# Attention scores of a decoder layer: two products of 128 rows per head, or three of 64 rows in paired halves of TensorE

## The chip, the cores and the metric

The kernel runs on one core of one Trainium2 chip. A core has TensorE (PE in the profile, with its weight loads listed as PEld), VectorE (DVE), ScalarE (ACT), GpSimd (POOL) and SyncE (SP), which issues most of the DMAs. The time is device microseconds of one execution, and the number that counts is the median over runs.

## The reference: what is computed

One decoder layer over 2048 positions of width 1024, in float32. Attention has 8 query heads of 64 and 2 key heads, each of which serves a group of 4 query heads; the window is 128 positions, and each head has a learned sink.

```python
h = rms_norm(x, attn_norm_g[l])
z = h @ w_in[l]
...
q = rms_norm(q, q_norm_g[l])
k = rms_norm(k, k_norm_g[l])
y_attn = swa_sink_attention(q, k, v, sinks[l])
y_conv = gate_b * short_conv(gate_c * xc, conv_w[l])
y = jnp.concatenate([rms_norm(y_attn, attn_out_g[l]),
                     rms_norm(y_conv, conv_out_g[l])], axis=-1)
x = x + y @ w_out[l]
hm = rms_norm(x, mlp_norm_g[l])
x = x + jnp.square(jax.nn.relu(hm @ w_up[l])) @ w_down[l]
```

Inside the attention, with blocks of 128 positions, the scores of a block of queries run over its own keys and those of the block before:

```python
sc = jnp.einsum('bnqhgd,bnkhd->bnhgqk', qb, kw).astype(jnp.float32) * scale
mask = (delta >= 0) & (delta < WINDOW) & (kpos[:, None, :] >= 0)
sc = jnp.where(mask[None, :, None, None], sc, NEG_INF)
```

## The kernel before

The products run on numbers of the type float32r. To keep the accuracy of float32, each operand is split into a high part (a copy in float32r) and a low part (what is left), and a product is a sum of part products: high by high, high by low, low by high. The helper `mm3` (lines 278 to 280) does that for the projections, with three products of 128 rows each.

The layer has two halves. In the first, the *mixers*, four chunks of 512 positions (`mixers`, each with four blocks of 128 positions) go through the input projection, attention, the convolution and the output projection. In the second, the MLP runs as Strassen products (lines 1454 and 1571); the diff does not touch it.

What a block does, in this order:

- `project_qkv` (for chunk 0, `first_chunk`) writes the projection `z` of its rows: 512 columns of q, 128 of k, 128 of v. The copy from PSUM is line 663 (line 627 for chunk 0).
- `qk_norm` normalises q and k.
- `qk_transpose` turns four 128x128 pieces of q into one bank (line 697) and k into another (line 699). A piece of q holds two heads that lie side by side, so both belong to the same key group, one on rows 0 to 63 and one on rows 64 to 127. Lines 702 and 703 make a tile `qt` in which every head has all 128 rows: its high part on one half, its low part on the other. Lines 704 to 707 do the same for k, in two arrangements (high over low, and low over high), for both key groups, in the tile `kw`, which keeps the own block and the one before.
- `softmax` makes the scores (line 724). Per pair of heads there is one bank; per head, two products of all 128 rows, one with each arrangement of k, and their sum holds all four part products. That is 16 products per block and 256 over the 16 blocks. They have 256 columns (own block and the one before), in block 0 128 columns. Line 732 copies the own half on ACT, line 735 puts the other block's scores where the mask says so, on DVE. Lines 737 to 749 are the softmax.
- `values` turns the probabilities (line 760) and multiplies them with v (line 812).

Attention's small products have other work beside them: `besides` is a generator of convolution, projection and normalisation steps for the same chunk and the next. `fill(n)` takes n steps of it, and the table FILL says how many stand between two parts of a block; PRIO gives parts a higher or lower rank. The framework's scheduler then sets the order of each engine's queue, by ranks and by its own costs, and that order is fixed in the program. In chunks 0 and 2 (blocks 0 to 3 and 8 to 11) the score products of a block stand together in TensorE's queue; in chunks 1 and 3 they stand one by one between the projections' products.

PSUM has eight banks: three for projections ("mm"), four that attention takes in turn ("at"), and one for turning ("tr").

Of the kernel before, what the change touches and what calls it, by code (L numbers as in the profile page):

```python
# [7 lines left out]
F32 = mybir.dt.float32  # L8
F32R = mybir.dt.float32r
BF16 = mybir.dt.bfloat16  # L10
I32 = mybir.dt.int32
AF = mybir.ActivationFunctionType
ALU = mybir.AluOpType
# [3 lines left out]
P = 128  # L17
# [3 lines left out]
HEADS, KVH, DH = 8, 2, 64  # L21
GQ = HEADS // KVH
AW = HEADS * DH
# [81 lines left out]
def hymba_layer(  # L105
# [19 lines left out]
    nc = tc.nc  # L125
# [30 lines left out]
    def bank(tag, name):  # L156
        return psum.tile([P, 512], F32, tag=tag, name=name, bufs=BANKS[tag])
# [5 lines left out]
    def zrow(name):  # L163

        return pool.tile([P, O_B], F32, tag="z", name=name, bufs=NT)


    ident = const.tile([P, P], F32, name="ident")
    mhalf = const.tile([P, 16], F32, name="mhalf")
# [3 lines left out]
        ident, ident, pattern=[[-1, P]], compare_op=ALU.is_equal, fill=0.0, base=0, channel_multiplier=1  # L173
# [3 lines left out]
    later = const.tile([P, P], I32, name="later")  # L177
    nc.gpsimd.memset(later, 1)
    nc.gpsimd.affine_select(
        later, later, pattern=[[1, P]], compare_op=ALU.is_gt, fill=0.0, base=0, channel_multiplier=-1  # L180
    )
    neg = const.tile([P, 1], F32, name="neg")
# [93 lines left out]
    def mm3(ps, st, mv, first, last):  # L276

        nc.tensor.matmul(ps, st(0), mv(0), start=first, stop=False)  # L278
        nc.tensor.matmul(ps, st(0), mv(1), start=False, stop=False)  # L279
        last_sum[0] = nc.tensor.matmul(ps, st(1), mv(0), start=False, stop=last).ins  # L280
# [116 lines left out]
    def parts(pool_, tag, name):  # L397
        return [pool_.tile([P, KD, CH], F32R, tag=f"{tag}{s}", name=f"{tag}{s}_{name}", bufs=1) for s in range(2)]
# [73 lines left out]
    z0 = [zrow(f"z0_{t}") for t in range(NT)]  # L472
# [3 lines left out]
    h = parts(pool, "h", "a0")  # L476
# [3 lines left out]
    rs0, rs0_2 = rs0_both[:, 0], rs0_both[:, 1]  # L480
# [37 lines left out]
    def first_chunk(first):  # L518
# [68 lines left out]
        pzs = [bank(tag, f"pz0_0_{t}") for t, tag in enumerate(("mm", "mm", "mm", "tr"))]  # L587
# [26 lines left out]
        for i in range(4):  # L614
            r = slice(i * 512, (i + 1) * 512)
# [3 lines left out]
        keep_q(0)  # L619
        w4 = [w.rearrange("p (k c) -> p k c", k=KD) for w in hl]  # L620
        for t in range(NT):
            nc.scalar.activation(z0[t][:, :AW], pzs[t], AF.Copy, scale=rs0[:, t : t + 1])
        for t in range(NT):
            ps = bank("at", f"pz0_1_{t}")[:, :256]
            hk = lambda s, k, t=t: h[s][:, k, t * P : (t + 1) * P]
# [7 lines left out]
    with tc.tile_pool(name="first", bufs=1) as first:  # L633
        with tc.manual_schedule(engines={ET.PE, ET.Activation, ET.DVE, ET.Pool, ET.SP}):
            rs0_in = first_chunk(first)

    with tc.tile_pool(name="mix_small", bufs=1) as mix_small, tc.tile_pool(name="mix", bufs=1) as mix:

        kw = mix.tile([P, 2, KVH, 2, P], F32R, name="kw")
        vz = mix.tile([P, 2, KVH, 2, 2, DH], F32R, name="vz")

        vd = mix.tile([P, KVH, 2, 2, DH], F32R, name="vd")
# [3 lines left out]
        def project_qkv(c, h, z):  # L648

            z += [zrow(f"z{c}_{t}") for t in range(NT)]  # L650
            both = [[by_k(w) for w in weights(None, c, f"q{half}")] for half in range(2)]
            w4 = [w.rearrange("p (k c) -> p k c", k=KD) for w in weights(None, c, "qkv2")]

            for pc, t in ((0, 0), (0, 1), (1, 0), (0, 2), (0, 3), (1, 1), (1, 2), (1, 3)):
                n = 256 if pc else AW
                ps = bank("mm", f"pz{c}_{pc}_{t}")[:, :n]
                hk = lambda s, k, t=t: h[s][:, k, t * P : (t + 1) * P]
                wk = (lambda s, k: w4[s][:, k, :]) if pc else (lambda s, k: both[k // (KD // 2)][s][:, k % (KD // 2), :])
                for k in range(KD):
                    mm3(ps, lambda s, k=k: hk(s, k), lambda s, k=k: wk(s, k), k == 0, k == KD - 1)  # L660
                    if (k % 2 or not pc) and k < KD - 1:
                        yield
                nc.scalar.copy(z[t][:, pc * AW : pc * AW + n], ps)
                if pc and not t:
                    qk_norm(c * NT, z[0])
                yield
# [22 lines left out]
        def qk_transpose(b, zt):  # L689

            nm = f"b{b}"
            own = b % 2
            lo, hi = slice(0, DH), slice(DH, P)
            qt = mix.tile([P, HEADS // 2, 2, P], F32R, tag="qt", name=f"qt_{nm}", bufs=1)
            pt = bank("at", f"ptq_{nm}")
            for j in range(4):
                nc.tensor.transpose(pt[:, j * P : (j + 1) * P], zt[:, j * P : (j + 1) * P], ident)
            pk = bank("at", f"ptk_{nm}")[:, :P]
            nc.tensor.transpose(pk, zt[:, O_K:O_V], ident)
            p3 = pt.rearrange("p (j q) -> p j q", j=4)  # L700
            for i, (a, o) in enumerate(((lo, hi), (hi, lo))):
                nc.scalar.copy(qt[a, :, i, :], p3[a])
                nc.vector.tensor_tensor(qt[o, :, i, :], p3[a], qt[a, :, i, :].bitcast(F32), op=ALU.subtract)
                nc.scalar.copy(kw[a, i, i, own, :], pk[a])
                nc.scalar.copy(kw[o, 1 - i, i, own, :], pk[a])
                nc.vector.tensor_tensor(kw[o, i, i, own, :], pk[a], kw[a, i, i, own, :].bitcast(F32), op=ALU.subtract)
                nc.vector.tensor_tensor(
                    kw[a, 1 - i, i, own, :], pk[a], kw[a, i, i, own, :].bitcast(F32), op=ALU.subtract
                )
            return qt  # L710

        def softmax(b, qt):


            nm = f"b{b}"
            nk = (2 if b else 1) * P
            own = b % 2
            sc = mix.tile([P, HEADS, P], F32, tag="sc", name=f"sc_{nm}", bufs=2)
            for pr in range(HEADS // 2):
                kv = pr * 2 // GQ  # L720
                ps = bank("at", f"psc_{nm}_{pr}").rearrange("p (h s k) -> p h s k", h=2, s=2)
                for j in range(2):
                    for r in range(2):
                        nc.tensor.matmul(  # L724
                            ps[:, j].rearrange("p s k -> p (s k)")[:, :nk],
                            qt[:, pr, j, :],
                            kw[:, r, kv, :, :].rearrange("p s k -> p (s k)")[:, :nk],
                            start=r == 0,
                            stop=r == 1,
                        )  # L730
                s2 = sc[:, pr * 2 : pr * 2 + 2, :]
                nc.scalar.copy(s2, ps[:, :, own, :])  # L732
                for j in range(2):
                    other = ps[:, j, 1 - own, :] if b else neg.to_broadcast([P, P])
                    nc.vector.copy_predicated(s2[:, j, :], later, other)  # L735
            ngm = mix_small.tile([P, HEADS], F32, tag="ngm", name=f"ngm_{nm}", bufs=2)
            nc.vector.tensor_reduce(ngm, sc, axis=AX.X, op=ALU.max, negate=True)
            nc.vector.tensor_tensor(ngm, ngm, nsink, op=ALU.min)  # L738
            den = mix_small.tile([P, HEADS], F32, tag="den", name=f"den_{nm}", bufs=2)
            for hd in range(HEADS):  # L740
                nc.scalar.activation(  # L741
                    sc[:, hd, :], sc[:, hd, :], AF.Exp, bias=ngm[:, hd : hd + 1], accum_out=den[:, hd : hd + 1]
                )
            es = mix_small.tile([P, HEADS], F32, tag="es", name=f"es_{nm}", bufs=2)
            nc.vector.tensor_tensor(es, sink, ngm, op=ALU.add)
            nc.scalar.activation(es, es, AF.Exp)
            nc.vector.tensor_tensor(den, den, es, op=ALU.add)
            nc.vector.reciprocal(den, den)
            nc.vector.tensor_tensor(sc, sc, den[:, :, None].to_broadcast([P, HEADS, P]), op=ALU.mult)
            return sc  # L750
# [227 lines left out]
        def besides(c, before, h, yt, rc, x1, h_next, z_next):  # L978
# [47 lines left out]
            if c + 1 < NCHUNK:  # L1026
                yield from project_qkv(c + 1, h_next, z_next)
            else:
                begin_mlp()
# [62 lines left out]
        z = z0  # L1092
# [6 lines left out]
        pr = bank("at", "pr")  # L1099
# [15 lines left out]
        for c in range(NCHUNK):  # L1115
            left, h, z = mixers(c, left, h, z)
# [215 lines left out]
    wts, ps, vs = {}, {}, {}  # L1332
# [105 lines left out]
    for i, (n, p) in enumerate(seq):  # L1438
# [12 lines left out]
        pt = ps[n, p if p in GOES_ON else AFTER.get(p)]  # L1451
        for k in range(NB):
            for j, (a, b) in enumerate(((0, 0), (0, 1), (1, 0))):
# [4 lines left out]
                    start=p not in GOES_ON and k + j == 0,  # L1458
                    stop=k + j == NB + 1,
# [93 lines left out]
    ps, vs = {}, {tb: {} for tb in range(NTB)}  # L1553

    later = []
    for i, (p, g) in enumerate(steps):
# [5 lines left out]
        for tb in range(NTB):  # L1562
            if first and p not in GOES_ON:
                ps[tb] = banks(tb, f"d{p}_{tb}")
            for j in range(NB):
# [3 lines left out]
                for k, n, cs in sums:  # L1569
                    a, b = ((0, 0), (0, 1), (1, 0))[n]  # L1570
# [4 lines left out]
                        start=first and p not in GOES_ON and k + n == 0,  # L1575
                        stop=last and k + n == 3,
# [34 lines left out]
```

## Time and profile before

The profile is of one execution; its span goes from the first to the last instruction. Each row of a view that shows a group of instructions has the line, the engine, what is written from what, the shapes, the count, and the busy time with the mean of one.

| | before |
|---|---|
| median of three runs | 1917.67 us (1916.55 to 1918.78) |
| span of the profiled execution | 1913.4 us |
| PE busy, granted clock | 1907.7 us, 1.00 |
| mixers, from the start to about | 690 us |
| products of the MLP | 609.7 + 609.5 us busy |
| score products (line 724) | 256, busy 49.0 us with overlaps |
| DVE, ACT, POOL busy | 1202.7, 829.4, 274.4 us |

TensorE is the engine to look at. [...] The other engines are idle for a third of the span and more.

### The profile page before, as it was taken

What the parts mean: (1) busy time and instruction counts of PE and PEld (TensorE: products, weight loads), DVE (VectorE), ACT (ScalarE), POOL (GpSimd) and SP (SyncE); (2) the same over time, 40 slices, a digit from 0 to 9 for tenths busy, and PEclk for the clock granted to TensorE, in tenths of its full rate; (3) what the DMA queues carried; (4) which work ended last, traced back from release to release, by engine and by line L of the source; (5) the groups of instructions that cost most, each with busy time, mean ns of one, the idle gap of its engine ahead of it and who ended that gap; (6) DMA issues with size and microseconds to landing.
All of it is one profiled execution on the core that took longest, in us unless ns stands there. A gap on an engine that the chain in (4) does not pass through costs nothing.

```text
span 1913.4 us, 24557 instructions
## 1 busy us (share of the span) xinstructions
PE 1907.7 (100%) x8930; PEld 1591.1 (83%) x8930; DVE 1202.7 (63%) x1857; ACT 829.4 (43%) x1557; POOL 274.4 (14%) x477
## 2 busy tenths in 40 slices
PE   9999999999999999999999999999999999999999
PEld 8888888888888888888888888888888888888887
DVE  5895567448467759998788766666534334457531
ACT  6564245335445346544555545453332332232320
POOL 2123212302221112233101111111000000100000
PEclk9999999999999999999999999999999999999999
DMA  9984844564578688777576544448954457766631
GB/s 305 333 320 120 329 189 177 213 227 160 203 266 277 215 294 251 221 215 244 195 233 213 175 145 159 140 148 321 364 198 150 138 171 224 281 228 213 217 124 55
DMA packets 232792, 413.80 MB, mean 216 GB/s; under 512 B 51672, under 2 KB 136416, under 8 KB 219872
## 3 DMA queue, kind: packets, MB, share of 16 engines
q1 hardware_dynamic: 203840, 336.59, 52.0%
q0 software_dynamic: 15424, 51.40, 6.9%
q10 hardware_dynamic: 13408, 24.26, 3.4%
q8 instruction: 70, 1.15, 0.2%
q14 instruction: 50, 0.41, 0.1%
HBM read 286.35 MB, written 125.83 MB: 215 GB/s over the span
## 4 chain that ended last, share of the span: by engine, by line
PE 99%; DVE 0%; POOL 0%; issue 0%; ACT 0%; DVEq 0%; POOLq 0%
PE u L1454 32%; PE d L1571 32%; PE pout L278 3%; PE pout L280 3%; PE pout L279 3%; PE pz L278 2%; PE pz L280 2%; PE pz L279 2%; PE psc_b L724 2%; PE pb_c L280 2%; PE pb_c L279 2%; PE pb_c L278 2%; PE px_c L278 2%; PE px_c L279 2%; PE px_c L280 2%; PE po_b L812 1%
## 5 line engine op out<-in xcount | busy, mean ns | idle before, releaser
L1454 PE MATMUL u<-op_x,wop 128*128 128x512 f32 x2688 | 609.7, 389 | 0.0
L1571 PE MATMUL d<-op_w,op_f 128*128 128x512 f32 x2691 | 609.5, 389 | 0.0
L1571 PEld LDWEIGHTS d<-op_w,op_f 128*128 128x128 f32 x2691 | 504.8, 188 | 104.7
L1454 PEld LDWEIGHTS u<-op_x,wop 128*128 128x128 f32 x2688 | 504.3, 188 | 105.3 <-issue 0.3
L434 DVE TENSOR_TENSOR op_f<-op_f 128x1024 fp32r<-128x1024 f32 x112 | 136.8, 1224 | 235.6 <-ACT op_f L433 235.4
L433 ACT CAST op_f<-op_f 128x1024 fp32r<-128x1024 f32 x112 | 117.7, 1051 | 349.5 <-DMA op_f<-fop 349.0
L452 ACT CAST wop<-wu 128x512 fp32r<-128x512 f32 x156 | 96.1, 619 | 92.0 <-PE u L1454 88.3
L453 DVE TENSOR_TENSOR wop<-wu,wop 128x512 fp32r<-128x512 f32 x156 | 110.2, 708 | 31.8 <-ACT wop L452 16.7
L1190 POOL DMA_DIRECT2D fop<-s x96 | 52.1, 542 | 443.2 <-DVE s L1193 436.7
L1196 DVE TENSOR_TENSOR u<-u,u 128x512 f32<-128x512 f32 x128 | 87.7, 685 | 19.4 <-PE u L1454 19.2
L434 DVE TENSOR_TENSOR op_w<-raw,op_w 128x1024 fp32r<-128x1024 f32 x56 | 68.3, 1221 | 28.8 <-ACT op_w L433 28.8
L433 ACT CAST op_w<-raw 128x1024 fp32r<-128x1024 f32 x56 | 58.8, 1052 | 48.4 <-PE d L1571 26.3
L1202 ACT ACTIVATE u<-u 128x512 f32<-128x512 f32 x64 | 40.5, 632 | 56.5 <-DVE u L1196 54.3
L741 ACT ACTIVATE sc_b<-sc_b,ngm_b 128x128 f32<-128x128 f32 x128 | 49.7, 389 | 30.0 <-DVE ngm_b L738 30.0
L773 POOL TENSOR_SCALAR_AFFINE_SELECT pp_b<-pp_b 128x512 fp32r<-128x512 f32 x60 | 41.3, 701 | 134.6 <-ACT pp_b L766 66.1
L1403 POOL DMA_DIRECT2D wds<-raw x16 | 8.5, 533 | 329.9 <-DVE raw L1401 329.9
L453 DVE TENSOR_TENSOR wop<-wu_s,wop 128x512 fp32r<-128x512 f32 x64 | 45.9, 718 | 11.9 <-ACT wop L452 11.7
L452 ACT CAST wop<-wu_s 128x512 fp32r<-128x512 f32 x64 | 39.4, 620 | 29.3 <-PE u L1454 24.9
L278 PE MATMUL pout<-w_wo,yt_c 128*128 128x512 f32 x128 | 51.5, 402 | 0.0
L280 PE MATMUL pout<-w_wo,yt_c 128*128 128x512 f32 x128 | 51.0, 398 | 0.0
L279 PE MATMUL pout<-w_wo,yt_c 128*128 128x512 f32 x128 | 50.2, 393 | 0.0
L735 DVE COPY_PREDICATED sc_b<-later,psc_b 128x128 f32<-128x128 int32 x120 | 29.4, 296 | 32.0 <-ACT sc_b L732 31.7
(265 smaller groups left out, 3119.0 us busy)
## 6 DMA issues: line engine op xcount, KB each, us to landing
op_f<-fop SPq DMA_DIRECT2D x112, 512.0 KB, 4.3
raw<-in_w_down_dram SPq DMA_DIRECT2D x72, 512.0 KB, 4.1
wu<-in_w_up_dram SPq DMA_DIRECT2D x128, 256.0 KB, 3.8
w_wo<-wo SPq DMA_DIRECT2D x24, 1024.0 KB, 6.7
fop<-s POOLq DMA_DIRECT2D x96, 256.0 KB, 2.6
fop<-u ACTq DMA_DIRECT2D x64, 256.0 KB, 2.6
op_x<-xop SPq DMA_DIRECT2D x28, 512.0 KB, 6.0
w_q<-q SPq DMA_DIRECT2D x12, 1024.0 KB, 6.7
```

The lines of the kernel that those rows point to most:

```text
L278: nc.tensor.matmul(ps, st(0), mv(0), start=first, stop=False)
L279: nc.tensor.matmul(ps, st(0), mv(1), start=False, stop=False)
L280: last_sum[0] = nc.tensor.matmul(ps, st(1), mv(0), start=False, stop=last).ins
L433: nc.scalar.copy(op[:, 0], raw)
L434: nc.vector.tensor_tensor(op[:, 1], raw, op[:, 0].bitcast(F32), op=ALU.subtract)
L452: splits.append(nc.scalar.copy(hi, blk).ins)
L453: lows.append(nc.vector.tensor_tensor(lo, blk, hi.bitcast(F32), op=ALU.subtract).ins)
L741: nc.scalar.activation(sc[:, hd, :], sc[:, hd, :], AF.Exp, bias=ngm[:, hd : hd + 1], accum_out=den[:, hd : hd + 1])
L1190: eng.dma_start(fop_dram[tb][ORDER_DOWN.index(i)][n // 2][:, n % 2], b)
L1196: return nc.vector.tensor_tensor(dst, ps, b, op=ALU.add).ins
L1454: nc.tensor.matmul(pt, wops[i][:, a, k, :], xops[tb, p][k // 2][:, b, k % 2, :], start=p not in GOES_ON and k + j == 0, stop=k + j == NB + ...
L1571: nc.tensor.matmul(ps[tb][j][:, cs], fs[tb][:, a, k, j * P : (j + 1) * P], w[:, b, k, cs], start=first and p not in GOES_ON and k + n == 0 ...
```

## The change

Each head's scores are now three products of 64 rows: high by high, high by low, low by high. The low by low product, which the sum of before had for nothing, is no longer made. A head uses the rows of its key group: group 0 lies on rows 0 to 63, group 1 on rows 64 to 127. For that, the copies of the projection (lines 627 and 663 of before) put q's columns in another order, so that a piece of 128 columns holds one head of each group, and turning it puts them on the two halves. `qt` and `kw` now hold high and low parts as two separate tiles over all 128 rows, so each is made by one copy and one subtraction. The products of the two groups alternate, each group with its own bank.

```diff
+    def by_kv(b):
+
+        return b.rearrange("p (v g d) -> p v g d", v=KVH, g=GQ)
+
+    def by_pair(zt):
+
+        return zt[:, :AW].rearrange("p (g v d) -> p v g d", v=KVH, g=GQ)
...
-            nc.scalar.activation(z0[t][:, :AW], pzs[t], AF.Copy, scale=rs0[:, t : t + 1])
+            nc.scalar.activation(by_pair(z0[t]), by_kv(pzs[t]), AF.Copy, scale=rs0[:, t : t + 1])
...
-        kw = mix.tile([P, 2, KVH, 2, P], F32R, name="kw")
+        kw = mix.tile([P, 2, 2, P], F32R, name="kw")
...
-                nc.scalar.copy(z[t][:, pc * AW : pc * AW + n], ps)
+                if pc:
+                    nc.scalar.copy(z[t][:, AW:], ps)
+                else:
+                    nc.scalar.copy(by_pair(z[t]), by_kv(ps))
...
-            qt = mix.tile([P, HEADS // 2, 2, P], F32R, tag="qt", name=f"qt_{nm}", bufs=1)
+            qt = mix.tile([P, 2, GQ, P], F32R, tag="qt", name=f"qt_{nm}", bufs=1)
...
-            for i, (a, o) in enumerate(((lo, hi), (hi, lo))):
-                nc.scalar.copy(qt[a, :, i, :], p3[a])
-                nc.vector.tensor_tensor(qt[o, :, i, :], p3[a], qt[a, :, i, :].bitcast(F32), op=ALU.subtract)
-                nc.scalar.copy(kw[a, i, i, own, :], pk[a])
-                nc.scalar.copy(kw[o, 1 - i, i, own, :], pk[a])
-                nc.vector.tensor_tensor(kw[o, i, i, own, :], pk[a], kw[a, i, i, own, :].bitcast(F32), op=ALU.subtract)
-                nc.vector.tensor_tensor(
-                    kw[a, 1 - i, i, own, :], pk[a], kw[a, i, i, own, :].bitcast(F32), op=ALU.subtract
-                )
+            p3 = pt.rearrange("p (g q) -> p g q", g=GQ)
+            nc.scalar.copy(qt[:, 0], p3)
+            nc.vector.tensor_tensor(qt[:, 1], p3, qt[:, 0].bitcast(F32), op=ALU.subtract)
+            nc.scalar.copy(kw[:, 0, own, :], pk)
+            nc.vector.tensor_tensor(kw[:, 1, own, :], pk, kw[:, 0, own, :].bitcast(F32), op=ALU.subtract)
...
-            for pr in range(HEADS // 2):
-                kv = pr * 2 // GQ
-                ps = bank("at", f"psc_{nm}_{pr}").rearrange("p (h s k) -> p h s k", h=2, s=2)
+            for g0 in range(0, GQ, 2):
+                pss = [bank("at", f"psc_{nm}_{g0}_{kv}").rearrange("p (h s k) -> p h s k", h=2, s=2) for kv in range(KVH)]
                 for j in range(2):
-                    for r in range(2):
-                        nc.tensor.matmul(
-                            ps[:, j].rearrange("p s k -> p (s k)")[:, :nk],
-                            qt[:, pr, j, :],
-                            kw[:, r, kv, :, :].rearrange("p s k -> p (s k)")[:, :nk],
-                            start=r == 0,
-                            stop=r == 1,
-                        )
+                    for n, (a, r) in enumerate(((0, 0), (0, 1), (1, 0))):
+                        for kv in range(KVH):
+                            rows = slice(kv * DH, (kv + 1) * DH)
+                            nc.tensor.matmul(
+                                pss[kv][:, j].rearrange("p s k -> p (s k)")[:, :nk],
+                                qt[rows, a, g0 + j, :],
+                                kw[rows, r].rearrange("p s k -> p (s k)")[:, :nk],
+                                start=n == 0,
+                                stop=n == 2,
+                            )
```

In the program the new products have a tile of 64x128 of the array, at row 0 or at row 64. The diff adds lines, so line 724 of before is 730 of after, 697 is 707, and 278 to 280 are 286 to 288.

**How the queues change.** The names in the rows below: `psc` with the block's number is a bank of scores (after it the pair of heads; in the new kernel the first head of the two, then the key group), `px`, `pb` and `pc` are the convolution's projections, `qt` and `kw` the operands of the scores.

The first place is TensorE's queue in block 1, where the score products end and the next projection goes on. Before:

```order
L724 MATMUL psc_b1_1_1004<-kw_631,qt_b1_942 128x256 x4
L724 MATMUL psc_b1_2_1012<-kw_631,qt_b1_942 128x256 x4
L724 MATMUL psc_b1_3_1020<-kw_631,qt_b1_942 128x256 x4
L278 MATMUL pb_c0_0_1_973<-h0_a0_250,w_wb0_0_904 128x512
L279 MATMUL pb_c0_0_1_973<-h1_a0_251,w_wb0_0_904 128x512
```

And now, the last two of its 24 score products:

```order
L730 MATMUL psc_b1_2_0_1008<-kw_631,qt_b1_942 128x256
L730 MATMUL psc_b1_2_1_1009<-kw_631,qt_b1_942 128x256
L286 MATMUL pb_c0_0_1_965<-h0_a0_250,w_wb0_0_904 128x512
L287 MATMUL pb_c0_0_1_965<-h1_a0_251,w_wb0_0_904 128x512
L288 MATMUL pb_c0_0_1_965<-h0_a0_250,w_wb0_1_905 128x512
```

The block's products stayed in one run at the same place: 16 before, four per bank, and now 24, in which the two key groups and their banks alternate. So it is in blocks 0 to 3 and 8 to 11, but for a few turned pieces that stand inside a run.

The second place is TensorE's queue in block 4, in chunk 1, where the scores begin. Before:

```order
L278 MATMUL px_c1_0_0_2469<-h0_h1_1425,w_wx01_0_2465 128x512
L279 MATMUL px_c1_0_0_2469<-h1_h1_1426,w_wx01_0_2465 128x512
L724 MATMUL psc_b4_0_2358<-kw_631,qt_b4_2289 128x256
L280 MATMUL px_c1_0_0_2469<-h0_h1_1425,w_wx01_1_2466 128x512
L724 MATMUL psc_b4_0_2358<-kw_631,qt_b4_2289 128x256
```

And now:

```order
L286 MATMUL px_c1_0_0_2469<-h0_h1_1425,w_wx01_0_2465 128x512
L287 MATMUL px_c1_0_0_2469<-h1_h1_1426,w_wx01_0_2465 128x512
L730 MATMUL psc_b4_0_0_2350<-kw_631,qt_b4_2289 128x256
L288 MATMUL px_c1_0_0_2469<-h0_h1_1425,w_wx01_1_2466 128x512
L730 MATMUL psc_b4_0_1_2351<-kw_631,qt_b4_2289 128x256
```

The projection's products still stand between the score products, so a pair of the two key groups is split by a product of all 128 rows. Over the whole program, 130 pairs stand side by side (95 of them in blocks 0 to 3 and 8 to 11), 124 score products do not have a partner beside them, and the queue goes over from 128 to 64 rows or back 314 times.

The third place is ACT's queue, where q and k of block 2 are copied. Before:

```order
L702 CAST qt_b2_1233<-ptq_b2_1234 64x4x128
L704 CAST kw_631<-ptk_b2_1239 64x128
L705 CAST kw_631<-ptk_b2_1239 64x128
L820 COPY o_b0_1222<-po_b0_1_1219 64x512
L702 CAST qt_b2_1233<-ptq_b2_1234 64x4x128
```

And now:

```order
L828 COPY o_b0_1222<-po_b0_0_1213 64x512
L711 CAST qt_b2_1233<-ptq_b2_1234 128x512
L713 CAST kw_631<-ptk_b2_1239 128x128
L828 COPY o_b0_1222<-po_b0_1_1219 64x512
L832 CAST at_b0_1227<-o_b0_1222 128x512
```

Of two copies for q and four for k, one each is left, and DVE's subtractions go the same way. The rest of the queues keeps its order but for neighbours that swap places.

More of the change, by code (lines that the diff above doesn't have):

```diff
@@ L692, in qk_transpose @@
             own = b % 2
-            lo, hi = slice(0, DH), slice(DH, P)
-            qt = mix.tile([P, HEADS // 2, 2, P], F32R, tag="qt", name=f"qt_{nm}", bufs=1)
+            qt = mix.tile([P, 2, GQ, P], F32R, tag="qt", name=f"qt_{nm}", bufs=1)
             pt = bank("at", f"ptq_{nm}")
-            for j in range(4):
-                nc.tensor.transpose(pt[:, j * P : (j + 1) * P], zt[:, j * P : (j + 1) * P], ident)
+            for g in range(GQ):
+                nc.tensor.transpose(pt[:, g * P : (g + 1) * P], zt[:, g * P : (g + 1) * P], ident)
             pk = bank("at", f"ptk_{nm}")[:, :P]
             nc.tensor.transpose(pk, zt[:, O_K:O_V], ident)
-            p3 = pt.rearrange("p (j q) -> p j q", j=4)
-            for i, (a, o) in enumerate(((lo, hi), (hi, lo))):
-                nc.scalar.copy(qt[a, :, i, :], p3[a])
-                nc.vector.tensor_tensor(qt[o, :, i, :], p3[a], qt[a, :, i, :].bitcast(F32), op=ALU.subtract)
-                nc.scalar.copy(kw[a, i, i, own, :], pk[a])
-                nc.scalar.copy(kw[o, 1 - i, i, own, :], pk[a])
-                nc.vector.tensor_tensor(kw[o, i, i, own, :], pk[a], kw[a, i, i, own, :].bitcast(F32), op=ALU.subtract)
-                nc.vector.tensor_tensor(
-                    kw[a, 1 - i, i, own, :], pk[a], kw[a, i, i, own, :].bitcast(F32), op=ALU.subtract
-                )
+            p3 = pt.rearrange("p (g q) -> p g q", g=GQ)
[3 more added lines that the diff above has]
+            nc.vector.tensor_tensor(kw[:, 1, own, :], pk, kw[:, 0, own, :].bitcast(F32), op=ALU.subtract)
             return qt
@@ L718, in softmax @@
             sc = mix.tile([P, HEADS, P], F32, tag="sc", name=f"sc_{nm}", bufs=2)
-            for pr in range(HEADS // 2):
-                kv = pr * 2 // GQ
-                ps = bank("at", f"psc_{nm}_{pr}").rearrange("p (h s k) -> p h s k", h=2, s=2)
+            for g0 in range(0, GQ, 2):
+                pss = [bank("at", f"psc_{nm}_{g0}_{kv}").rearrange("p (h s k) -> p h s k", h=2, s=2) for kv in range(KVH)]
                 for j in range(2):
-                    for r in range(2):
-                        nc.tensor.matmul(
-                            ps[:, j].rearrange("p s k -> p (s k)")[:, :nk],
-                            qt[:, pr, j, :],
-                            kw[:, r, kv, :, :].rearrange("p s k -> p (s k)")[:, :nk],
-                            start=r == 0,
-                            stop=r == 1,
-                        )
[L731 to L735, printed above, removed]
+                    for n, (a, r) in enumerate(((0, 0), (0, 1), (1, 0))):
[8 more added lines that the diff above has]
+                            )
+                for kv in range(KVH):
+                    ps = pss[kv]
+                    s2 = sc[:, kv * GQ + g0 : kv * GQ + g0 + 2, :]
+                    nc.scalar.copy(s2, ps[:, :, own, :])
+                    for j in range(2):
+                        other = ps[:, j, 1 - own, :] if b else neg.to_broadcast([P, P])
+                        nc.vector.copy_predicated(s2[:, j, :], later, other)
             ngm = mix_small.tile([P, HEADS], F32, tag="ngm", name=f"ngm_{nm}", bufs=2)
```

## The prediction

> **What bounds the kernel now.** I read the page first: the summary, the slices and the chain.
>
> ```profile
> span 1913.4 us, 24557 instructions
> PE 1907.7 (100%) x8930; PEld 1591.1 (83%) x8930; DVE 1202.7 (63%) x1857; ACT 829.4 (43%) x1557; POOL 274.4 (14%) x477
> PE   9999999999999999999999999999999999999999
> PEclk9999999999999999999999999999999999999999
> PE 99%; DVE 0%; POOL 0%; issue 0%; ACT 0%; DVEq 0%; POOLq 0%
> ```
>
> PE is busy in every slice, at the full granted clock, and the chain that ended last is PE for 99%. The page warns that a busy PE need not be PE at its peak, so I asked the waits of PE alone, and then the groups by line for the rest of the table.
>
> ```profile
> PE idle L579 <- POOL ident L172: 1.6, 1, 1.6
> ```
>
> That is the whole answer: one wait of 1.6 us, at the very start. No matmul of the mixers waits for ACT, DVE or a DMA long enough to be seen. So the end is set by the sum of what the matmuls take in TensorE's queue, one after the other, and I call that a matmul's **slot**: from its start to the next start. The durations of the records (389 ns for a product of 512 columns) are no slots, because records overlap. The chain in order of time gives the slot:
>
> ```profile
> 690.66 609.56 PE u L1454 x2688
> ```
>
> 609.56 / 2688 = 0.227 us for 512 columns. For the score products (line 724) I asked the timeline of PE at block 2, at block 0 and at block 5.
>
> ```profile
> 109.57 2.08 PE L724 MATMUL psc_b<-kw,qt_b 128*128 128x256 f32 x16
> 111.48 0.40 PE L278 MATMUL pb_c<-h_a,w_wb 128*128 128x512 f32 x1
> ...
> 59.93 1.90 PE L724 MATMUL psc_b<-kw,qt_b 128*128 128x128 f32 x16
> 61.67 0.45 PE L278 MATMUL px_c<-h_a,w_wx 128*128 128x512 f32 x1
> ...
> 243.24 0.28 PE L724 MATMUL psc_b<-kw,qt_b 128*128 128x256 f32 x1
> 243.35 0.40 PE L278 MATMUL pb_c<-h_h,w_wb 128*128 128x512 f32 x1
> 243.59 0.28 PE L724 MATMUL psc_b<-kw,qt_b 128*128 128x256 f32 x1
> 243.70 0.40 PE L279 MATMUL pb_c<-h_h,w_wb 128*128 128x512 f32 x1
> 243.94 0.28 PE L724 MATMUL psc_b<-kw,qt_b 128*128 128x256 f32 x1
> ```
>
> In a run, 16 products of 256 columns take 111.48 - 109.57 = 1.91 us, 0.12 us each. In block 0, which has no block before it, the products have 128 columns, and 16 of them take 61.67 - 59.93 = 1.74 us, 0.109 us each: half the columns, and yet 91% of the slot. What the two forms share is one load of 128 columns of weights per product, so I read 0.109 us as the floor that a weight load sets (an estimate from these two rows). Between products of 512 columns, two score products and two others take 243.94 - 243.24 = 0.70 us; less 2 x 0.227, a score product costs 0.123 us there too. All 256 of them therefore take 240 x 0.12 + 16 x 0.109 = 30.5 us of the span, and nothing else that the diff touches is on the path.
>
> **The change part by part.**
>
> ```profile
> L724 PE MATMUL psc_b<-kw,qt_b x256: 220/282/368, 59.9 to 629.7; 128*128 128x256 f32 x120, 128*128 128x128 f32 x8
> L735 DVE COPY_PREDICATED sc_b<-later,psc_b x120: 246/297/309, 80.5 to 630.9; 128x128 f32<-128x128 int32 x120
> L732 ACT COPY sc_b<-psc_b x64: 349/373/405, 61.2 to 630.0; 128x256 f32<-128x256 f32 x64
> ```
>
> *The products.* Per block, 16 products of 128 rows become 24 of 64 rows, of the same columns: 256 become 384. In the new order on PE, 95 pairs (the same step for the two key groups) stand in blocks 0 to 3 and 8 to 11, where almost all 24 products stand in one run. In the other eight blocks the scheduler puts products of 512 columns between them, as it did before: 35 pairs stand together there, and 124 products stand alone, either the partner or nothing of their kind beside them. So even if two halves of the rows work at the same time at no price, 130 + 124 = 254 slots replace 256.
>
> What a half-row product costs is not in this trace, since every product in it has 128 rows. Low bound: it shares a slot with its partner, 0.06 us each. High bound: a slot of its own, 0.12 us. I take the slot of its own, for the reason of block 0: the slot hardly fell with half the work, the weight load of 128 columns is paid per product, and there are 128 more of them. Then the scores take 360 x 0.12 + 24 x 0.109 = 45.8 us: **+15.3 us**. Something between is possible: the streams of a pair overlap, but the loads come one after the other. Then the 95 pairs in runs cost 2 x 0.109 each, the 35 others and the 124 single products 0.12 (their loads lie beside 0.227 us of other work): 20.7 + 4.2 + 14.9 = 39.8 us, +9.3 us.
>
> *The turns between full and half rows.* 314 times a product of one kind follows one of the other. No row shows such a turn. It cannot save time, since the columns still stream. High bound: the next product waits until the record of the last one ends. The record's mean here is 0.284 us against a slot of 0.12, so 0.164 us, and 314 x 0.164 = 51.5 us. The nearest row, products of 256 columns between those of 512, changes shape at every step for 0.003 us, so I take 0 and keep 51.5 for the range.
>
> The two bounds together are 45.8 - 15.5 (130 shared slots) + 0 for the low end and 45.8 + 51.5 for the high one.
>
> *Turning and splitting q and k* (lines 697 to 709).
>
> ```profile
> L702 ACT CAST qt_b<-ptq_b x32: 562/581/583, 45.2 to 620.1; 64x512 fp32r<-64x512 f32 x32
> L704 ACT CAST kw<-ptk_b x32: 256/259/262, 45.7 to 620.6; 64x128 fp32r<-64x128 f32 x32
> L703 DVE TENSOR_TENSOR qt_b<-ptq_b,qt_b x32: 683/689/694, 52.0 to 620.9; 64x512 fp32r<-64x512 f32 x32
> L707 DVE TENSOR_TENSOR kw<-ptk_b,kw x32: 274/289/295, 52.9 to 621.8; 64x128 fp32r<-64x128 f32 x32
> ```
>
> Before, a block has two copies of 0.581 and four of 0.259 us on ACT, 2.20 us, and two and four subtractions on DVE, 2 x 0.689 + 4 x 0.289 = 2.53 us. After, one of each size, over 128 partitions with the same columns: 0.84 and 0.98 us. Over 16 blocks ACT loses 22 us and DVE 25 us of work. I cost it at nothing: PE waited for neither, and its order is written, so a result that is ready earlier lets nothing start earlier.
>
> *The scattered copy of q* (lines 627 and 663): the same elements to other places, 16 copies.
>
> ```profile
> L663 ACT COPY z<-pz x24: 362/481/594, 157.0 to 528.9; 128x512 f32<-128x512 f32 x12, 128x256 f32<-128x256 f32 x12
> ```
>
> Even at twice its 0.59 us it lies beside matmuls, and it comes a block or more ahead of the scores. Nothing; without that cover, 16 x 0.59 = 9 us.
>
> *What comes later.* The scores now fill two banks at a time, so the first copy starts after six products of each bank. The tightest place is block 4, whose probabilities are turned (line 760) soonest after its scores:
>
> ```profile
> 242.16 1.23 DVE L749 TENSOR_TENSOR sc_b<-sc_b,den_b 128x1024 f32<-128x1024 f32 x1
> ...
> 248.94 1.03 PE L760 MATMUL ptp_b<-ident,sc_b 128*128 128x128 f32 x8
> ```
>
> Softmax ends at 243.39 us and is wanted at 248.94: 5.6 us of slack. The new order brings the two 1 to 2 us nearer. It holds. In blocks 4, 8 and 12 the turn of the next block's q now stands among the second half of the scores, and its bank is the one of the first half: it needs that half's copy (0.373 us) and two masked copies (0.297 us each), 0.97 us, and some 1.6 us of matmuls stand between. I take 0, at worst 3 x 0.97 = 2.9 us. Behind it in PE's queue stand the block's other scores, and the next projection. On SP a few loads swap places with a neighbour; PE waited for no load, and the waits view says the same of stores, so 0.
>
> **The sum.** 1913.4 + 15.3 = 1928.7 us of span. The median of the three runs shown, 1917.67, lies 4.3 us above that span (launch, and what lies around it). So **1933 us**, with 1927 (loads alone in series) to 1936 (with the bank waits) as the forecast's own range.
>
> **The rivals.**
>
> *Pairs side by side, at no price: not slower.* Each of the 130 pairs takes one slot, 30.5 becomes 30.3 us, and the time is 1917.5. For it: different rows and different banks, so nothing is shared but the queue. Against it: 0.109 us of a weight load per product, which no row shows two at a time. It decides where the loads of both halves go at once; if they only half do, the time is between this and 1927. [...]
>
> *Each turn between full and half rows costs.* With the price at 0.02 to 0.164 us, 6 to 51 us come on top: 1924 to 1969 us if pairs share a slot, 1939 to 1984 if they do not; 0.09 us, in the middle, gives 1946 and 1961. For it: 314 turns, most of them around single products, and 0.164 us of record after the slot. Against it: PE changes between columns of 128, 256 and 512 without a gap. [...]
>
> *A single half-row product goes beside its neighbours.* If the 124 single ones cost 0.06 us and pairs a slot, 30.3 - 7.4 = 22.9 us, and the time is 1910. It decides from about 0.09 us per single product. Nothing speaks for it: the neighbours use all the rows.
>
> **How the numbers follow.** Forecast 0.40, pairs at no price 0.24, paid turns 0.29, single products beside 0.07. 0.2% is 3.8 us, about what a measurement of this kernel tells from no change. The forecast and the paid turns are slower by more, together 0.69, and 0.02 of the pairs that only half overlap: 0.71. The pairs at no price are within it, 0.21, with 0.01 faster: 0.08 with the last rival. The range takes in the pairs (1917.5, less their 3.8), the forecast, and two thirds of the paid turns: 1914 to 1960. Left out are the last rival and the dearer turns, 0.17.
>
> **What would show it.** In block 2 the 24 products, from the first start to the next product of 512 columns: 2.87 us if each has its slot, 1.44 us if pairs share, more by the price of two turns. In block 5, single products between those of 512 columns: 0.35 us per step as now, or that and two turns. Waits on PE should stay near 1.6 us. I am wrong if the starts within a pair lie a few ns apart, if a step in block 5 is well over 0.35 us, or if PE waits for ACT or DVE in the mixers.

## The result, and the profile after

The changed kernel takes 2020.12 us (median of four runs), the kernel of before 1918.22 in the same comparison: a ratio of 1.055, with a 95% interval of 1.052 to 1.057. It is slower by 102 us. The span of the profiled execution is 2018.4 us, 105.0 us more than before. The page of the changed kernel, from the same parts as before:

```profile
span 2018.4 us, 24688 instructions
PE 2002.8 (99%) x9058; PEld 1619.0 (80%) x9058; DVE 1178.8 (58%) x1793; ACT 808.9 (40%) x1493; POOL 275.7 (14%) x477
PE   9999999999999999999999999999999999999999
PEclk9999998899997899999999999999999999999999
```

PE is still busy throughout, but the granted clock is no longer 9 everywhere: it falls to 8 and 7 in chunks 1 and 3. The MLP's two groups take what they took (610.3 and 609.5 us busy, 609.7 and 609.5 before), so all of the loss lies in the mixers. The busy share, 100% before and 99% now, can't say more. The timeline of PE does, first in block 2, where the 24 products stand in one run:

```profile
108.93 0.39 PE L288 MATMUL pb_c<-h_a,w_wb 128*128 128x512 f32 x1
109.25 1.69 PE L730 MATMUL psc_b<-kw,qt_b 64*128 64x256 f32 x24
110.86 0.50 PE L286 MATMUL pb_c<-h_a,w_wb 128*128 128x512 f32 x1
111.20 0.40 PE L287 MATMUL pb_c<-h_a,w_wb 128*128 128x512 f32 x1
```

24 products take 110.86 - 109.25 = 1.61 us, less than the 1.91 us of 16 full ones. Inside that row, the trace has the two starts of a pair 3 ns apart and one pair 0.118 us behind the other: a pair does share a slot. But the product ahead of the run has a slot of 0.32 us where 0.227 was usual, and the one behind it 0.34. In block 5, where single products stand between those of 512 columns, first PE and then the weight loads:

```profile
257.20 0.38 PE L730 MATMUL psc_b<-kw,qt_b 64*128 64x256 f32 x1
257.51 0.49 PE L288 MATMUL pb_c<-h_h,w_wb 128*128 128x512 f32 x1
257.94 0.38 PE L730 MATMUL psc_b<-kw,qt_b 64*128 64x256 f32 x1
...
263.79 0.58 PE L730 MATMUL psc_b<-kw,qt_b 64*128 64x256 f32 x1
264.30 0.79 PE L287 MATMUL pb_c<-h_h,w_wb 128*128 128x512 f32 x1
265.02 0.58 PE L730 MATMUL psc_b<-kw,qt_b 64*128 64x256 f32 x1
```

```profile
257.20 0.18 PEld L730 LDWEIGHTS psc_b<-kw,qt_b 64*128 64x128 f32 x1 [0.25 <-issue]
257.51 0.19 PEld L288 LDWEIGHTS pb_c<-h_h,w_wb 128*128 128x128 f32 x1
257.94 0.18 PEld L730 LDWEIGHTS psc_b<-kw,qt_b 64*128 64x128 f32 x1 [0.24 <-issue]
```

A step of one score product and one of 512 columns takes 257.94 - 257.20 = 0.74 us; before it took 0.35. The weight load now starts with its own product (257.20 and 257.20), in both directions. Before, it started 0.22 us ahead of it, under the product before:

```profile
243.02 0.19 PEld L724 LDWEIGHTS psc_b<-kw,qt_b 128*128 128x128 f32 x1
243.24 0.19 PEld L278 LDWEIGHTS pb_c<-h_h,w_wb 128*128 128x128 f32 x1
```

The first of these rows is the load for the score product at 243.24 us, the second that of the product of 512 columns behind it, at 243.35. So at each turn between 128 and 64 rows the load is no longer hidden, and (0.74 - 0.35) / 2 = 0.19 us are paid per turn. Some us later the same step takes 265.02 - 263.79 = 1.23 us. The windows of the changed kernel say why (columns: PE busy, the other engines, the granted clock, DMA):

```profile
229.00:246.20 17.20, 17.20 (x54) 8.83 (x53) 3.49 (x10) 1.02 (x3) 0.18 (x1) 1.00 0.61 251
262.10:268.90 6.80, 6.80 (x15) 3.70 (x15) 1.00 (x4) 0.74 (x2) 0.00 (x0) 0.50 0.00 0
215.00:390.00 175.00, 174.21 (x673) 121.43 (x673) 71.91 (x147) 53.73 (x154) 20.16 (x42) 0.90 0.39 152
```

Block 4 (the first row) runs at full clock and needs 17.2 us from its first score product to its last. Before it needed 6.6, with 8 score products and 5 products of 512 columns fewer in between, which are 2.1 us of the difference; the other 8.5 us go with its turns. At 262 us (the second row) the clock is half. In all, the trace has nine stretches at half clock in the mixers, together 82 us: eight amid such turns, and one of 3.4 us that begins as the wait at line 841 ends. The waits of PE, one row before, are now these (the row of `idle` apart, all are new, and two of 0.5 and 0.3 us are left out):

```profile
PE pa_b L841 <- DVE o_b L836: 3.4, 1, 3.4
PE pt_a L314 <- DVE h_h L319: 2.2, 2, 1.6
PE pout L286 <- DVE x L971: 1.7, 2, 1.3
PE idle L587 <- POOL ident L180: 1.6, 1, 1.6
PE pt_a L314 <- DVE ms_b L843: 1.2, 1, 1.2
PE ptq_b L707 <- DVE sc_b L743: 0.8, 1, 0.8
```

Three things, then, can have cost the 102 us: the turns, the clock, and waits for DVE that were not there before. The number of products, which the prediction went by, is a fourth.

### The profile page after: what moved, and what is told of

Same layout as the page of the kernel before. It is cut to its first block, busy times and chain, and to the rows that moved or that the text cites. A ratio compares the mean times of both kernels' runs of the same rounds, so it can differ in the third digit from the quotient of the medians.

```text
span 2018.4 us, 24688 instructions
## 1 busy us (share of the span) xinstructions
PE 2002.8 (99%) x9058; PEld 1619.0 (80%) x9058; DVE 1178.8 (58%) x1793; ACT 808.9 (40%) x1493; POOL 275.7 (14%) x477
## 4 chain that ended last, share of the span: by engine, by line
PE 45%; issue 4%; POOL 1%; DMA 0%; ACT 0%; DVE 0%; DVEq 0%; POOLq 0%
PE d L1579 30%; PE u L1462 14%; POOL fop L1198 0%; DMA fop<-s 0%; POOL st_m L1136 0%; DVE s L1201 0%; ACT u L1210 0%; ACT u L1207 0%; DVE u L1204 0%; ACT u L1217 0%; DVE d L1522 0%; DVEq L1614 0%; POOLq L1198 0%; ACT op_x L441 0%; DVEq L1201 0%
## 5 line engine op out<-in xcount | busy, mean ns | idle before, releaser
L1462 PE MATMUL u<-op_x,wop 128*128 128x512 f32 x2688 | 610.3, 389 | 0.3 <-ACT u L1217 0.3
L1579 PE MATMUL d<-op_w,op_f 128*128 128x512 f32 x2691 | 609.5, 389 | 0.0
L730 PEld LDWEIGHTS psc_b<-kw,qt_b 64*128 64x128 f32 x384 | 44.5, 200 | 46.1 <-issue 44.7
L730 PE MATMUL psc_b<-kw,qt_b 64*128 64x256 f32 (+1 forms) x384 | 79.6, 358 | 0.0
L740 ACT COPY sc_b<-psc_b 128x256 f32<-128x256 f32 x64 | 22.0, 375 | 112.6 <-PE psc_b L730 112.4
L286 PE MATMUL pout<-w_wo,yt_c 128*128 128x512 f32 x128 | 52.4, 409 | 0.3 <-DVE x L971 0.3
```

The source lines that it names most:

```text
L730: nc.tensor.matmul(pss[kv][:, j].rearrange("p s k -> p (s k)")[:, :nk], qt[rows, a, g0 + j, :], kw[rows, r].rearrange("p s k -> p (s k)")[ ...
L1462: nc.tensor.matmul(pt, wops[i][:, a, k, :], xops[tb, p][k // 2][:, b, k % 2, :], start=p not in GOES_ON and k + j == 0, stop=k + j == NB + ...
L1579: nc.tensor.matmul(ps[tb][j][:, cs], fs[tb][:, a, k, j * P : (j + 1) * P], w[:, b, k, cs], start=first and p not in GOES_ON and k + n == 0 ...
```

## The experiments

The theory is that the turns between 128 and 64 rows cost the time, 0.19 us each and more where they lower the clock. The rivals are the greater number of products, and the new order of copies, banks and queues. All ratios are against the kernel of before on the same chip.

**Full rows for the changed program.** The order, copies and banks stay; the products read all 128 rows.

```diff
-                            rows = slice(kv * DH, (kv + 1) * DH)
+                            rows = slice(0, P)
```

> The changed program with its order, copies and banks, but every score product reads all 128 rows (so it sums the scores of two heads, which are not the reference's). Turns theory (each turn between 128 and 64 rows costs about 0.19 us at full clock, 314 of them, and the gaps lower the granted clock): no turn is left, 384 products of a slot each, 1917.7 + 128 x 0.12 = 1933 us, clock 1.00, PE waits under 5 us. Rival, the new order (banks in pairs, scattered copy, later softmax): 2005 to 2020 us, as the changed kernel. Rival, the number of products alone: 1933 us too, but then it cannot tell of the other 87.

Measured: 1944.5 us, ratio 1.014 (1.013 to 1.016). The turns are gone, and with them some 75 of the 102 us, though the shared slots are gone too. In block 2 the 24 products now take a slot each:

```profile
111.29 3.04 PE L730 MATMUL psc_b<-kw,qt_b 128*128 128x256 f32 x24
114.17 0.40 PE L286 MATMUL pb_c<-h_a,w_wb 128*128 128x512 f32 x1
```

114.17 - 111.29 = 2.88 us, just what the prediction's forecast said of half-row products. But 1933 was missed by 11 us, and PE's waits are 9.8 us beside the first one, not under 5. So the rival of the new order holds a part.

**Half rows for the kernel of before.** Its 16 products per block are cut to the first 64 rows; nothing is paired, and queues and copies stay.

```diff
-                            qt[:, pr, j, :],
-                            kw[:, r, kv, :, :].rearrange("p s k -> p (s k)")[:, :nk],
+                            qt[:DH, pr, j, :],
+                            kw[:DH, r, kv, :, :].rearrange("p s k -> p (s k)")[:, :nk],
```

> The kernel of before with its 256 score products cut to rows 0 to 63 (the low part of one head and the high part of the other are left out of each sum). Turns theory: the queue turns 226 times, 226 x 0.19 = 43 us, and the clock is halved in chunks 1 and 3 as in the changed kernel: 1960 to 2000 us, clock under 0.99. Rival, number of products: 1918 us. Rival, the new order: 1918 us.

Measured: 1960.8 us, ratio 1.023 (1.022 to 1.025), at the low end of the expectation. Its only wait on PE is the 1.6 us at the start, as before. In block 4 a step takes 229.06 - 228.33 = 0.73 us:

```profile
228.33 0.38 PE L724 MATMUL psc_b<-kw,qt_b 64*128 64x256 f32 x1
228.64 0.49 PE L280 MATMUL px_c<-h_h,w_wx 128*128 128x512 f32 x1
229.06 0.38 PE L724 MATMUL psc_b<-kw,qt_b 64*128 64x256 f32 x1
```

The same number of products in the same order, and 45 us more. The four runs tell the turns from the clock. Two of them, 1958.06 and 1958.18 us, had a mean granted clock of 1.000: they are 41.8 us above the 1916.3 of before, 0.185 us for each of the 226 turns. The other two, 1963.5 and 1964.9 us, had 0.997 and 0.996. The profile is of the last one; its clock was halved for 17.1 us in the mixers, less than I had thought, and it is 6.8 us longer than the first two, 0.40 us for each us at half clock. Where a run of score products stands alone, as between block 1 and block 2, the lag behind the kernel of before grows by 0.37 us, two turns of 0.185.

**The score products in runs.** Two ranks of the changed kernel (second number of PRIO's second and fourth row: the scores of chunks 1 and 3) are set to 0. 42 turns are left of 314.

```diff
-    (220, -60, -60, -50, 40, 0, 20, 40, -60, 280, 0, 0, 0, 0),
+    (220, 0, -60, -50, 40, 0, 20, 40, -60, 280, 0, 0, 0, 0),
...
-    (200, 20, 180, 240, 0, 0, 40, 40, 240, 0, 0, 30, 0, 0),
+    (200, 0, 180, 240, 0, 0, 40, 40, 240, 0, 0, 30, 0, 0),
```

> The changed kernel with two ranks set to 0 (chunks 1 and 3, scores), so that nearly every block's 24 score products stand in one run: 42 turns instead of 314, 188 to 192 pairs. Turns theory: 192 slots for 256, -7.7 us, and 42 x 0.19 = +8 us: 1918 us, 1914 to 1921, clock 1.00. Rival, number of products: 1933 us. Rival, the new order of copies and banks: over 1950 us.

Measured: 1935.0 us, ratio 1.010 (1.008 to 1.011): 85 us better than the changed kernel, but 14 us over the upper end of the expectation. The largest waits of PE in this kernel:

```profile
PE pt_m L382 <- DVE xt_m L383: 3.7, 2, 2.5
PE pa_b L841 <- DVE o_b L836: 3.4, 1, 3.4
PE pt_a L314 <- DVE h_h L319: 2.9, 3, 1.8
```

With the smaller ones they are 15.0 us, beside the 1.6. By the sum of the expectation the turns and the shared slots cancel; the waits were not in it.

**The same two ranks for the kernel of before.** The same edit on the kernel with full rows.

> The kernel of before with the same two ranks set to 0: its 16 products per block stand in runs too. Turns theory: no half rows, no turns to pay, 1917 us, 1914 to 1921. Rival, that runs alone help or hurt: off by more than 4 us, which would then have to be taken from the run with half rows as well.

Measured: 1918.1 us, ratio 1.0008 (0.9999 to 1.0017), no change that can be told. Runs alone neither help nor hurt; what they spare is the turns. The profiled run, the longest of its eleven with 1921.8 us, has 4.3 us of waits on PE that before did not have, the largest 2.5 us at line 833: a part of the 15.0 us above may come with the ranks.

**Both groups in one half.** The kernel with runs, where each product reads rows 0 to 63.

```diff
-                            rows = slice(kv * DH, (kv + 1) * DH)
+                            rows = slice(0, DH)
```

> The kernel with runs (1935 us), but the products of both key groups read rows 0 to 63, so the second group's scores are not the reference's. Same number of turns (42). Theory that a pair shares a slot because its halves of the rows differ: nothing is shared, 192 more slots of 0.12 us, +23 us: 1954 to 1962 us, and 24 products in a run take 2.9 us where they took 1.6. Rival, that half rows alone make a product cheap: 1935 us and 1.6 us.

Measured: 1949.4 us, ratio 1.017 (1.016 to 1.019). Block 2 of this kernel, and of the kernel with runs:

```profile
113.67 3.12 PE L730 MATMUL psc_b<-kw,qt_b 64*128 64x256 f32 x24
116.72 0.50 PE L286 MATMUL pb_c<-h_a,w_wb 128*128 128x512 f32 x1
```

```profile
110.79 1.69 PE L730 MATMUL psc_b<-kw,qt_b 64*128 64x256 f32 x24
112.41 0.50 PE L286 MATMUL pb_c<-h_a,w_wb 128*128 128x512 f32 x1
```

3.05 us against 1.62: in one half nothing is shared. That is 16 x 1.43 = 23 us, as expected. The total rose by 14 only, 5 us short of the expectation. Most of what is missing lies in the waits: PE, now later, waited 8.2 us where it had waited 15.0.

**One group after the other.** The kernel with runs, with the two groups' products of a step no longer in turn: six of one bank, then six of the other.

```diff
-                for j in range(2):
-                    for n, (a, r) in enumerate(((0, 0), (0, 1), (1, 0))):
-                        for kv in range(KVH):
+                for kv in range(KVH):
+                    for j in range(2):
+                        for n, (a, r) in enumerate(((0, 0), (0, 1), (1, 0))):
```

> The kernel with runs, both halves used, but all six products of one key group's bank come first and then the six of the other, instead of in turn. If a partner must stand right beside it: 1952 to 1960 us, 2.7 to 2.9 us a run. If TensorE looks further ahead in its queue: 1935 us, 1.6 us a run.

Measured: 1938.5 us, ratio 1.011 (1.010 to 1.013). Block 2:

```profile
109.86 2.03 PE L730 MATMUL psc_b<-kw,qt_b 64*128 64x256 f32 x24
111.83 0.50 PE L286 MATMUL pb_c<-h_a,w_wb 128*128 128x512 f32 x1
```

1.97 us, far nearer to 1.62 than to 3.05. The queue of this kernel has the six products of a bank together, and still 18 of the 24 starts in the trace come in pairs 5 to 10 ns apart; the six others stand near the front and at the end of the run. The partner need not stand beside. That the two of such a pair lie in different halves is read from the 0.12 us between starts in one half (24 products in 3.05 us); the trace does not name the half.

**202 turns.** The changed kernel with both ranks at 150: some blocks of chunks 1 and 3 in runs, some one by one.

> The changed kernel with both ranks of the scores set to 150: half the blocks of chunks 1 and 3 in runs, half one by one, 202 turns. Turns theory with the clock: between the kernel with runs (42 turns, 1935) and the changed one (314 turns, 2020) by turns, 85/272 = 0.31 us each: 1985 us, 1970 to 2000, with some 30 to 60 us at half the clock. Turns theory without the clock: 160 x 0.19 = 30 us over 1935: 1965 us and no more half clock than there. Rival, waits that come with any new order: no relation to the turns, 1930 to 1950.

Measured: 1988.3 us, ratio 1.037 (1.036 to 1.039), as the theory with the clock had it. A window of a one-by-one stretch in it:

```profile
199.60:223.50 23.90, 23.90 (x50) 13.66 (x50) 8.07 (x20) 5.61 (x12) 2.56 (x3) 0.50 0.45 149
```

The clock is half for 23.9 us on end, though PE is busy in every us by its records; chunk 3 has such a stretch as well, and 58 us in all are at half. So 42, 202 and 314 turns give 1935, 1988 and 2020 us, 0.28 to 0.33 us per turn. Of that, 0.19 are the turn at full clock; the rest is the clock and a few us of shared slots, since the pairs that stand side by side fall from 190 to 149 and 130. From 42 to 202 turns, 160 x 0.19 + 41 x 0.12 and 40% of the 51 us more at half clock are 56 us, for 53 measured.

**One wait moved.** In the kernel with runs, DVE's queue had the scaling of block 11's q and k (line 695), which waits for POOL, ahead of block 7's last sum (line 836), for which PE waits at line 841:

```profile
375.02 0.83 DVE L695 TENSOR_TENSOR z<-z,rq_b 128x640 f32<-128x640 f32 x1 [2.21 <-POOL rq_b L201]
375.76 0.28 DVE L836 TENSOR_TENSOR o_b<-o_b 128x128 f32<-128x128 f32 x1
```

In the changed kernel it is the same, at 417.95 and 418.69 us. In the kernel of before the sum stood six places ahead of the scaling (364.16 and 368.86 us), so in DVE's queue more than neighbours changed places. An edge puts the scaling behind:

```diff
-            nc.vector.tensor_tensor(zqk, zqk, rq[:, :, None].to_broadcast([P, nh, DH]), op=ALU.mult)
+            with tc.issue_after(o_sums[b - NT]) if b == 11 else nullcontext():
+                nc.vector.tensor_tensor(zqk, zqk, rq[:, :, None].to_broadcast([P, nh, DH]), op=ALU.mult)
...
-                nc.vector.tensor_tensor(o[:, :P], o[:, :P], o[:, P : 2 * P], op=ALU.add)
+                o_sums[b] = nc.vector.tensor_tensor(o[:, :P], o[:, :P], o[:, P : 2 * P], op=ALU.add).ins
```

> The kernel with runs and one edge on DVE: the first scaling of the normalised q and k of block 11 is queued behind the last sum of block 7, as it stands in the kernel of before. Theory that the new waits of PE come from the order that the scheduler gives DVE and ACT: the wait of 3.4 us of PE for that sum (line 841) is gone, and the time is 3 us less than the kernel with runs. Rival, that DVE is simply late there: the wait stays.

Measured: 1930.8 us, ratio 1.007 (1.006 to 1.009); the kernel with runs had 1.010. In the waits of PE the row is down from 3.4 to 0.5 us:

```profile
PE pa_b L843 <- DVE o_b L838: 0.5, 1, 0.5
```

The gain is 4.2 us by the medians, a little over the wait: behind it, the kernel with runs had 3.4 us at half clock (from 376.75 us), and that stretch is gone too. So this wait came from the place in the queue, not from a DVE that is short of time.

No version beat the kernel of before. By these sums, a kernel with runs and without the new waits would come out about level with it; no run shows that.

## Why the prediction was wrong

All three signs of being wrong that the prediction named came: starts 3 ns apart in a pair, 0.74 us for a step of block 5, and waits for DVE.

**What bounds the kernel**: right. The sum of slots on PE sets the end, and the 105.0 us of span can be laid out on it. The count of products: +15.3 us, as computed (in block 2, 2.88 us of full rows for 1.91). Shared slots of 130 pairs: -15.5. 314 turns at 0.185 us: +58.1. New waits, and the clock that falls behind them: the full-row kernel has 29.9 us over the span of before, of which 15.3 are the count, so 14.6; 9.8 of that are its waits, and 10.2 us behind or within them were at half clock. What is left of 75.1 us between the changed and the full-row kernel, 75.1 - 58.1 + 15.5 = 32.5 us, I put down to the clock. That last is a remainder; what speaks for it is that 72 us more than in the full-row kernel are at half clock, where a step takes 1.23 us instead of 0.74, so that 40% of the time is lost. 40% of 72 is 29 us, and the half-row run of before lost the same 40%, 6.8 us of 17.1.

**A slot of its own for each half-row product**: wrong. The step was "I take the slot of its own, for the reason of block 0". Block 0 had shown 0.109 us per product with half the columns; I read that as the floor of a weight load, and took it that two loads can't go at once. In two halves they do: in block 2 the two loads of a pair start 3 to 4 ns apart and take 0.18 us each, and a pair takes 0.118 us, where a single product takes 0.12 in one half. The rival "pairs side by side" was right in this.

**The turns**: this is the step that failed by size, a term of 0 that measured 58 us. I took 0, on the ground that a change from 512 to 256 columns costs 0.003 us, and held 0.164 us for the worst. But in the rows both of those products have the form 128*128, and a turn changes it to 64*128; no row of before had a turn in it, and the nearest row was of another kind. The rival that turns cost was right in kind, though dearer than its dearest price. The bound was too low as well: it counted the time that a product's record outlasts its slot, but not the weight load, which starts only with its product after a turn (both at 257.20 us in block 5; the load takes 0.18 us). Measured: 0.185 to 0.19 us per turn; within a pair, where the half changes and the form 64*128 stays, the starts lie 3 ns apart.

**The clock**: not in the sum at all. Every row of before had 1.00, and I never asked what turns would do to it. By the sum above it is the largest part of the 51 us by which the time lies over the dearest rival with shared pairs (1969 us); the new waits and a turn dearer than 0.164 us are the rest. It also differs between runs of one kernel: the longest run of the changed kernel, 2031.6 us, had 0.973, and the other three, near 2020, 0.979 to 0.981.

**ACT and DVE at nothing**: wrong in sign. Most of the 22 and 25 us of work did go (ACT 829.4 to 808.9, DVE 1202.7 to 1178.8 us busy), and PE got new waits for DVE of some 10 us. "Its order is written" was said of PE's queue; I did not ask how DVE's own order would move. Work that waits for POOL came ahead of a sum that PE wants, as the moved wait shows for 3.4 us of it. That the four subtractions less per block moved it there is likely, but no run shows it. The other waits were not tried one by one. The kernel of before with half rows, which kept its copies and order, had none, so half rows alone don't make them.

**Softmax's slack and the bank of q**: the slack held: PE has no wait for the probabilities. The bank did cost, 0.8 us at line 707, within the 2.9 allowed.

## What to carry to other kernels

Count how often TensorE's queue goes from one shape of the array to another before cutting products to half rows: each turn cost 0.19 us here, more than the 0.12 us that a shared slot saves. Even in a run there is little to win: in the kernel with runs, the 24 products of block 2 take 1.62 us for 1.91 before, and the products ahead and behind take 0.2 us more, so 0.1 us is left. Where a scheduler deals out single products, the run has to be kept together: here 42 turns gave 1935 us and 314 gave 2020. And work taken off an idle engine was not free here, where a scheduler sets the queues (3.4 us of PE's waits in one place): look at what moved up in the queue, and what it waits for.

## What the runs showed of the hardware that was not expected

The two halves of the rows need no alternating queue: with six products of one half ahead of six of the other, 24 took 1.97 us, against 1.62 in turn and 3.05 in one half. The granted clock fell to half while PE's records show it busy all the time, in stretches of 6.8 to 20.5 us in the changed kernel and of 23.9 us in the one with 202 turns, where turns follow each other, and also where PE had waited a few us (3.4 us in the full-row kernel, with 6.8 us at half that begin within the wait). The nine stretches in the changed kernel's mixers last 3.41 us (one), 6.83 (four), 10.24 (three) and 20.48 (one). One program kept its clock in two executions and lost some of it in two others: the half-row runs of before had 1.000 twice, 0.997 and 0.996. What exactly the clock goes by is left open: no run kept the turns and their gaps apart.
